# 960 unused matrix products of many shapes behind the needed ones, in a two-layer float32 trunk

## The chip, the core and the metric

The kernel runs on one core of one Trainium2 chip. Its engines are named as the profile names them: PE is TensorE (matmuls), PEld the loading of a matmul's stationary operand (its weights), DVE is VectorE, ACT ScalarE, POOL GpSimd, and SP issues DMAs. The metric is the device time of one execution in microseconds (us).

## The reference

Two post-LN residual layers on 272 tokens (16 learned meta tokens and 256 frames; the pad slots in front of them are masked and stay out of the kernel), with 2048 features. The first layer mixes by gated linear attention and stick-breaking attention, the second by a Mamba-2 scan. Cut to its frame:

```python
for layer in range(DEPTH):                      # DEPTH = 2
    if layer % 2 == 0:
        f = _even_mixer(h, valid, ...)          # h @ w_in, GLA and stick-breaking heads, gates, @ w_out
    else:
        f = _odd_mixer(h, valid, ...)           # h @ w_in, conv, chunked scan, gates, @ w_out
    ...                                         # h = layer norm of the residual sum
# the meta tokens are dropped: the output is (1, 256, 2048) float32
```

Nearly all arithmetic is in the four projections: 2048 features to some 10,000 columns and back in each layer, for 272 tokens.

## The kernel before

**Projections.** All weights are packed into units of 128 x 2048 numbers that are loaded one after the other (`raw`, three buffers), and each half of a unit is split into a high and a low part (`split_into`, L146 on ACT and L147 on DVE or POOL). Both parts have type float32r, in which PE takes a number with fewer bits. A float32 product is made of three float32r products: high by high, high by low, low by high. `three` (L164 to L166) issues them for the input projections and for layer 0's output projection, with 128 weight columns and 256 to 274 moving columns; `out1_half` (L422 to L424) issues them for layer 1's output projection with 512, and in the last two groups 256, moving columns. The activations lie in two row buffers, `xhi` and `xlo`, of 16 x 320 numbers per partition.

**Mixers.** Between the projections stand smaller products. Most of them have plain float32 operands, which PE takes apart by itself: such a matmul leaves two records in the trace and float32r one. Shapes are written as the profile writes them: `128*64 128x256` is 128 rows of contraction, 64 weight columns, and 256 moving columns.

**PSUM.** Eight banks of 512 float32 columns: four `pj` buffers for projections, two `po` buffers, and two fixed banks `z0`, `z1`.

**Order.** Mixers are generators that are pushed to a list and advanced one step (`tick`) between pieces of a projection. The framework then lists each engine's instructions by its own simulation, keeps dependences, and puts in the semaphore waits; a buffer that is taken again waits for the work on its former content.

**The end.** `tail` does the last four units of layer 1's output projection. For units 1 and 2 of them the split parts are put into `xhi` and `xlo`, whose content is no longer needed by then. Then it normalizes and stores the 256 tokens in two halves: `bn_stats` and the affine part on DVE, ACT and POOL, and DMAs to `out_h`.

At the start, before any data is there, ten products of constants are issued whose result is never read (L232).

Of the kernel before, what the change touches and what calls it, by code (L numbers as in the profile page):

```python
# [6 lines left out]
F32 = mybir.dt.float32  # L7
# [5 lines left out]
P = 128  # L13
# [54 lines left out]
NU = len(L0) + len(L1)  # L68
# [20 lines left out]
class _Body:  # L89
# [1014 lines left out]
    def tail(self):  # L1104

        nc, lp = self.nc, self.lp
        vec, pool = nc.vector, nc.gpsimd
        i0, g = NU - 4, NG - 1
        self.drain()
        self.load_unit(i0 + 2)  # L1110
        for n, dq in enumerate((1, 2)):
            for h in range(2):
                src = self.raw[i0 + dq][:, h * 1024 : (h + 1) * 1024]
                o = slice((2 * n + h) * 1024, (2 * n + h + 1) * 1024)
                hi, lo = [a.rearrange("p k t -> p (k t)")[:, o] for a in self.xrows]
                nc.scalar.activation(hi, src, AF.Copy)
                vec.tensor_tensor(lo, src, hi.bitcast(F32), op=ALU.subtract)
                self.parts[i0 + dq, h] = (hi, lo)
            if n == 0:
                self.load_unit(i0 + 3)  # L1120
        lg = self.hp.tile([P, D], F32, tag="hacc", name="lg")
        lb = lp.tile([P, D], F32, tag="M", name="lb")
        nc.sync.dma_start(lg, self.lnr_d[0].partition_broadcast(P))
        nc.sync.dma_start(lb, self.lnr_d[1].partition_broadcast(P))
        for h in range(2):
            self.split_half(i0 + 3, h)
        for t in range(2):
            st = lp.tile([P, 8, 6], F32, tag="fst", name=self.nm("fst"), bufs=2)
            acc = self.acc[:, t, :]
            for dq in range(4):  # L1130
                halves = (0, 1) if t == 1 and dq == 3 else (None,)
                for b in halves:
                    ps = self.pj()
                    for h in range(2):
                        self.out1_half(ps, g, t, *self.parts[i0 + dq, h], h, b)
                    self.out1_add(ps, g, t, dq, b)
                    with self.tc.high_priority():
                        for c in range(2) if b is None else (b,):
                            vec.bn_stats(st[:, 2 * dq + c, :], acc[:, dq * 512 + c * 256 : dq * 512 + (c + 1) * 256])
            mv = lp.tile([P, 2], F32, tag="fmv", name=self.nm("fmv"), bufs=2)  # L1140
            v, r, tm, mr = [lp.tile([P, 1], F32, tag=f"f{n}", name=self.nm("f"), bufs=2) for n in range(4)]
            with self.tc.high_priority():
                vec.bn_aggr(mv, st)
                vec.tensor_scalar(v, mv[:, 1:2], LN_EPS, None, op0=ALU.add)
                nc.scalar.activation(r, v, AF.Ln)
                nc.scalar.activation(r, r, AF.Exp, scale=-0.5)
                self.newton(r, v, tm)
                vec.scalar_tensor_tensor(mr, mv[:, 0:1], -1.0, r, op0=ALU.mult, op1=ALU.mult)
            cut = (0, 1024, 2048) if t == 0 else (0, 384, 1216, 2048)
            ch = [slice(a, b) for a, b in zip(cut, cut[1:])]  # L1150
            for cs in ch[1:]:
                vec.scalar_tensor_tensor(acc[:, cs], acc[:, cs], mv[:, 0:1], lg[:, cs], op0=ALU.subtract, op1=ALU.mult)
            a = acc[:, ch[0]]
            nc.scalar.activation(a, a, AF.Identity, bias=mr, scale=r)
            pool.tensor_tensor(a, a, lg[:, ch[0]], op=ALU.mult)
            pool.tensor_tensor(a, a, lb[:, ch[0]], op=ALU.add)
            for cs in ch[1:]:
                vec.scalar_tensor_tensor(acc[:, cs], acc[:, cs], r, lb[:, cs], op0=ALU.mult, op1=ALU.add)
                nc.sync.dma_start(self.out[t * P : (t + 1) * P, cs], acc[:, cs])
            nc.sync.dma_start(self.out[t * P : (t + 1) * P, ch[0]], a)  # L1160


def _pack(i):
# [53 lines left out]
```

## Time and profile before

| what | us |
|---|---|
| time, median of 2 runs | 1436.1 (1435.95 to 1436.24) |
| the profiled execution's own time | 1439.71 |
| its span, first to last instruction | 1437.6 |
| PE busy | 1418.9 (99%) |
| DVE busy | 984.4 (68%) |
| ACT busy | 761.5 (53%) |
| POOL busy | 350.1 (24%) |

The mean granted TensorE clock is 0.995 of full. In a row of the timeline the first number is the start in us from the span's start, the second the length in us; `x2` is two records in one row. A matmul's record is longer than its share of PE, since the next one starts before it ends: the distance from one start to the next is its cost in a dense sequence. In a row of the windows stand the stretch, its length, busy time and count of PE, PEld, DVE, ACT and POOL, then the granted TensorE clock, and the share and GB/s of DMA.

### The profile page before, as it was taken

Reading aid. Unit: us, or ns where it says so; the run is one execution under the profiler, and the core shown is the slowest. Engines: PE = TensorE matmul, PEld = TensorE weight load, DVE = VectorE, ACT = ScalarE, POOL = GpSimd, SP = SyncE. Lnnn points to the kernel's source line nnn. Section 1 sums busy time; section 2 is a strip of 40 time slices with the busy share of each in tenths; the row PEclk is TensorE's granted clock in tenths of the full one; section 3 lists DMA queues with packets and bytes.
Section 4 is the critical chain, followed back from the end, with each engine's and each line's share of the span. In section 5 each row is a group of like instructions: output and inputs, shape, how many; then the busy total and the mean of one; then the engine's idle time right before and its main releaser. Section 6 shows DMA issues by size and latency. Waiting matters only on the chain.

```text
span 1437.6 us, 26048 instructions
## 1 busy us (share of the span) xinstructions
PE 1418.9 (99%) x10780; PEld 1345.8 (94%) x10780; DVE 984.4 (68%) x1516; ACT 761.5 (53%) x1126; POOL 350.1 (24%) x297
## 2 busy tenths in 40 slices
PE   9999999999999999999999999999999999999996
PEld 7999999999999999999999999899898998989985
DVE  8647575575564465447799978577776767767677
ACT  5535454454345444445587666565555555555651
POOL 5010000100101110014401435333433433434333
PEclk9999999999999999999999999999999999999998
DMA  7544545445444445443446564554544556445551
GB/s 261 206 167 159 169 153 167 157 152 174 168 156 172 147 143 179 162 147 128 141 144 218 184 213 165 205 211 166 217 165 167 215 176 217 153 168 184 203 209 58
DMA packets 36566, 249.82 MB, mean 174 GB/s; under 512 B 4128, under 2 KB 4960, under 8 KB 7776
## 3 DMA queue, kind: packets, MB, share of 16 engines
q1 hardware_dynamic: 36304, 247.90, 49.4%
q8 instruction: 84, 1.38, 0.4%
q14 instruction: 34, 0.28, 0.1%
q10 hardware_dynamic: 144, 0.26, 0.1%
HBM read 245.94 MB, written 2.20 MB: 173 GB/s over the span
## 4 chain that ended last, share of the span: by engine, by line
PE 94%; DVE 3%; issue 1%; ACT 1%; POOL 1%; DMA 0%; POOLq 0%; SPq 0%; DVEq 0%
PE pj L164 24%; PE pj L166 24%; PE pj L165 24%; PE pj L422 4%; PE pj L423 4%; PE pj L424 4%; PE po L1070 1%; DVE wlo L147 1%; DVE xlo L737 1%; PE po L1072 1%; PE po L1023 1%; PE po L1074 0%; DMA raw<-in_wts 0%; ACT whi L146 0%; PE po L508 0%
## 5 line engine op out<-in xcount | busy, mean ns | idle before, releaser
L164 PE MATMUL pj<-xhi,whi 128*128 128x272 f32 (+4 forms) x2560 | 737.5, 288 | 3.9 <-DVE fix L815 2.5
L165 PE MATMUL pj<-xlo,whi 128*128 128x272 f32 (+4 forms) x2560 | 733.6, 287 | 0.0
L166 PE MATMUL pj<-xhi,wlo 128*128 128x272 f32 (+4 forms) x2560 | 733.1, 287 | 0.0
L147 DVE TENSOR_TENSOR wlo<-raw,whi 128x1024 fp32r<-128x1024 f32 (+1 forms) x402 | 511.3, 1275 | 289.2 <-ACT whi L146 288.1
L146 ACT ACTIVATE whi<-raw 128x1024 fp32r<-128x1024 f32 (+1 forms) x432 | 452.5, 1049 | 407.0 <-PE pj L165 344.1
L164 PEld LDWEIGHTS pj<-xhi,whi 128*128 128x128 f32 x2560 | 483.5, 189 | 8.4 <-DVE fix L815 2.9
L165 PEld LDWEIGHTS pj<-xlo,whi 128*128 128x128 f32 x2560 | 482.6, 189 | 2.1 <-DVE xlo L293 0.7
L166 PEld LDWEIGHTS pj<-xhi,wlo 128*128 128x128 f32 x2560 | 482.3, 188 | 2.2 <-DVE xlo L293 1.3
L164 PE MATMUL pj<-mixh,whi 128*128 128x272 f32 x384 | 111.6, 292 | 0.0
L165 PE MATMUL pj<-mixl,whi 128*128 128x272 f32 x384 | 110.5, 288 | 0.0
L166 PE MATMUL pj<-mixh,wlo 128*128 128x272 f32 x384 | 110.2, 287 | 0.0
L147 POOL TENSOR_TENSOR wlo<-raw,whi 128x1024 fp32r<-128x1024 f32 x30 | 75.2, 2508 | 136.0 <-ACT whi L146 136.0
L422 PE MATMUL pj<-whi,yh 128*128 128x512 f32 (+1 forms) x244 | 97.3, 399 | 0.0
L423 PE MATMUL pj<-wlo,yh 128*128 128x512 f32 (+1 forms) x244 | 94.9, 389 | 0.0
L424 PE MATMUL pj<-whi,yl 128*128 128x512 f32 (+1 forms) x244 | 94.3, 386 | 0.0
L253 POOL TENSOR_TENSOR gr<-gr,gsc 128x1088 f32<-128x1088 f32 x6 | 15.5, 2578 | 290.4 <-ACT gsc L252 290.4
L165 PEld LDWEIGHTS pj<-mixl,whi 128*128 128x128 f32 x384 | 72.3, 188 | 0.3
L164 PEld LDWEIGHTS pj<-mixh,whi 128*128 128x128 f32 x384 | 72.1, 188 | 0.5
L166 PEld LDWEIGHTS pj<-mixh,wlo 128*128 128x128 f32 x384 | 72.3, 188 | 0.1
L431 DVE SCALAR_TENSOR_TENSOR acc<-pj,rr,acc 128x512 f32<-128x512 f32 (+1 forms) x65 | 47.4, 737 | 28.4 <-PE pj L424 28.2
L1078 POOL TENSOR_TENSOR yu<-yu,gz 128x256 f32<-128x256 f32 x32 | 44.0, 1382 | 84.6 <-DVE yu L1077 77.5
L424 PEld LDWEIGHTS pj<-whi,yl 128*128 128x128 f32 x244 | 45.9, 188 | 9.8
(305 smaller groups left out, 1519.1 us busy)
## 6 DMA issues: line engine op xcount, KB each, us to landing
raw<-in_wts SPq DMA_DIRECT2D x214, 1024.0 KB, 4.8
ebc<-edr SPq DMA_DIRECT2D x8, 1664.0 KB, 6.9
hacc<-in_xT SPq DMA_DIRECT2D x8, 272.0 KB, 6.3
raw<-in_wts SPq DMA_DIRECT2D x8, 256.0 KB, 5.3
lg<-in_lnr SPq DMA_DIRECT2D x1, 1024.0 KB, 4.4
lb<-in_lnr SPq DMA_DIRECT2D x1, 1024.0 KB, 5.9
out_h<-acc SPq DMA_DIRECT2D x2, 512.0 KB, 2.6
out_h<-acc SPq DMA_DIRECT2D x2, 416.0 KB, 2.5
```

Of the source, the lines that this page charges most:

```text
L146: self.nc.scalar.activation(hi, src, AF.Copy)
L147: eng.tensor_tensor(lo, src, hi.bitcast(F32), op=ALU.subtract)
L164: mm(ps, whi, xhi, start=first, stop=False)
L165: mm(ps, whi, xlo, start=False, stop=False)
L166: mm(ps, wlo, xhi, start=False, stop=last)
L253: mul(c, c, e, op=ALU.mult)
L422: mm(ps, yh[:, kk, tt], hi[:, k, :], start=kk == 0, stop=False)
L423: mm(ps, yh[:, kk, tt], lo[:, k, :], start=False, stop=False)
L424: mm(ps, yl[:, kk, tt], hi[:, k, :], start=False, stop=kk == 3)
L431: self.nc.vector.scalar_tensor_tensor(a, ps, r[:, t : t + 1], a, op0=ALU.mult, op1=ALU.add)
L737: vec.scalar_tensor_tensor(self.xlo[:, d, :T], x, g, self.xhi[:, d, :T].bitcast(F32), op0=ALU.mult, op1=ALU.subtract)
L1078: nc.gpsimd.tensor_tensor(u, u, z[:, j, :], op=ALU.mult)
```

## The change

`tail` calls a new method, `rest`, as its last step. It issues 960 matmuls in 53 groups ("patterns"). A group takes one `po` buffer (or two) and makes `rep` = 6 times three products (the last group 8 times three), each with operands that lie in SBUF already: weights are slices of the last unit's high and low part (`wh`, `wl`), moving operands slices of the row buffers (`xh`, `xl`). Nothing reads the results. `n` is the number of moving columns, `kk` of rows (contraction), `m` of weight columns; `po` is the first PSUM column, `xo` the place of the moving operand in its row; `blk` takes the moving operand in two pieces, `two` writes the result in two pieces; `f32` takes the operands as plain float32; `alt` puts the results into the lower and the upper 64 PSUM partitions in turn.

```diff
             nc.sync.dma_start(self.out[t * P : (t + 1) * P, ch[0]], a)
+        self.rest()
+
+    def rest(self):
+
+        mm = self.nc.tensor.matmul
+        xh, xl = [a.rearrange("p k t -> p (k t)") for a in self.xrows]
+        wh, wl = self.parts[NU - 1, 0]
+
+        def pattern(n, xo=48, kk=P, m=P, po=0, banks=1, alt=False, two=0, f32=False, rep=6, blk=None, xp=320, mp=0):
+            pss = [self.po() for _ in range(banks)]
+            for k in range(rep):
+                hi, lo = [t[:kk, k * P : k * P + m] for t in (wh, wl)]
+                p, q = [t[:kk, xo + k * xp : xo + k * xp + n] for t in (xh, xl)]
+                if blk:
+                    p, q = [
+                        t[:kk, xo + k * xp : xo + k * xp + blk[1] * 2].rearrange("p (a b) -> p a b", a=2)[:, :, : blk[0]]
+                        for t in (xh, xl)
+                    ]
+                for i, (s, v) in enumerate([(hi, p), (hi, q), (lo, p)]):
+                    if f32:
+                        s, v = s.bitcast(F32), v.bitcast(F32)
+                    c = 3 * k + i
+                    r = slice(64 * (c % 2), 64 * (c % 2) + m) if alt else slice(mp, mp + m)
+                    o = pss[c % banks][r, po : po + n]
+                    if two:
+                        o = pss[0][r, po : po + 2 * two].rearrange("p (a b) -> p a b", a=2)[:, :, : n // 2]
+                    elif blk:
+                        o = o.rearrange("p (a b) -> p a b", a=2)
+                    mm(o, s, v, start=c < 2, stop=c >= 3 * rep - 2, skip_group_check=True)
+
+        for n in (16, 32, 64, 128, 144, 160, 192, 208, 224, 240, 248, 254):
+            pattern(n)
+        for xo in (0, 16, 32):
+            pattern(144, xo=xo)
+        for n, kk in ((144, 16), (144, 48), (144, 80), (272, 16), (272, 80), (16, 16), (16, 80)):
+            pattern(n, kk=kk)
+        for n, m in ((16, 16), (144, 16), (272, 16), (144, 64), (256, 64)):
+            pattern(n, m=m)
+        for po in (16, 64, 112, 128, 176, 240):
+            pattern(272, po=po)
+        pattern(272, banks=2)
+        pattern(256, banks=2)
+        pattern(512, xo=0, xp=512, banks=2)
+        pattern(272, blk=(136, 144))
+        pattern(272, blk=(136, 160), xp=384)
+        pattern(272, two=144)
+        pattern(272, two=160)
+        for n in (16, 64, 128, 144, 256, 272):
+            pattern(n, f32=True)
+        for n, m in ((144, 64), (256, 64)):
+            pattern(n, m=m, f32=True, alt=True)
+        for n, kk in ((16, 16), (16, 64), (144, 16), (144, 64)):
+            pattern(n, kk=kk, f32=True)
+        pattern(272, rep=8)
```

On DVE, ACT, POOL and SP the instructions are the same as before. PE's queue ended, before, with the last products of the output projection (`pj`, the numbers are buffers) and a branch.

```order
L424 MATMUL pj_15657<-whi_15500,yl_15128 128x256
L422 MATMUL pj_15657<-whi_15504,yh_15127 128x256
L423 MATMUL pj_15657<-wlo_15505,yh_15127 128x256
L424 MATMUL pj_15657<-whi_15504,yl_15128 128x256
L1212 UNCONDITIONAL_BRANCH
```

In the changed kernel the same products are followed by `rest`; the waits of an instruction stand in brackets, and PE_49 is PE's own semaphore.

```order
L422 MATMUL pj_15657<-whi_15504,yh_15127 128x256
L423 MATMUL pj_15657<-wlo_15505,yh_15127 128x256
L424 MATMUL pj_15657<-whi_15504,yl_15128 128x256
L1189 MATMUL po_15695<-xhi,whi_15500 128x16 [waits PE_49]
L1189 MATMUL po_15695<-xlo,whi_15500 128x16
L1189 MATMUL po_15695<-xhi,wlo_15501 128x16
```

All 960 stand behind the last needed product, and only the first product into a buffer has a wait. Of the groups with two buffers, the queue of the changed kernel has this at the change from the first buffer to the second.

```order
L1189 MATMUL po_16322<-xhi,whi_15500 128x272
L1189 MATMUL po_16322<-xhi,wlo_15501 128x272
L1189 MATMUL po_16322<-xlo,whi_15500 128x272
L1189 MATMUL po_16323<-xlo,whi_15500 128x272
L1189 MATMUL po_16323<-xhi,whi_15500 128x272
L1189 MATMUL po_16323<-xhi,wlo_15501 128x272
```

The code takes the two buffers in turn; the queue has nine products into the first and then nine into the second.

## The prediction

> **What bounds the kernel now.** The page comes first, for what the span is made of.
>
> ```profile
> span 1437.6 us, 26048 instructions
> PE 1418.9 (99%) x10780; PEld 1345.8 (94%) x10780; DVE 984.4 (68%) x1516; ACT 761.5 (53%) x1126; POOL 350.1 (24%) x297
> PE 94%; DVE 3%; issue 1%; ACT 1%; POOL 1%; DMA 0%; POOLq 0%; SPq 0%; DVEq 0%
> ```
>
> PE is busy for 99% of the span and 94% of the chain that ended last is PE. Whatever stands on PE's queue is paid in full, unless it falls where PE would be idle. The timeline of the last 12 us shows the one large stretch of that kind.
>
> ```profile
> 1426.15 0.28 PE L424 MATMUL pj<-whi,yl 128*128 128x256 f32 x1
> ...
> 1426.39 0.28 PE L423 MATMUL pj<-wlo,yh 128*128 128x256 f32 x1
> ...
> 1426.51 0.28 PE L424 MATMUL pj<-whi,yl 128*128 128x256 f32 x1
> 1426.83 0.48 DVE L431 SCALAR_TENSOR_TENSOR acc<-pj,rr,acc 128x256 f32<-128x256 f32 x1 [0.48 <-PE pj L424]
> ...
> 1434.62 0.33 SPq L1160 DMA_DIRECT2D out_h<-acc  x1
> ```
>
> PE's last matmul starts at 1426.51 and ends at 1426.8; the other engines then normalize and store until 1437.6. That is 10.8 us without PE work. The run behind this profile took 1439.71 us, 2.1 more than its span and 3.6 more than the median of 1436.1.
>
> **The change part by part.** Nothing is removed or moved. 960 matmuls stand behind the last one on PE, and no instruction is added on another engine. Their operands (xhi, xlo, and the last unit's whi and wlo) are complete when PE's own last products have read them. The only new waits are PE's on itself: the first product into a PSUM buffer waits for the group that used that buffer before, at least nine products earlier, so the awaited one has ended by the time its turn comes; I cost them at nothing (a wait that did bite would cost one drain, about the 0.28 us of a record, for 56 of them 16 us at most). So the added work starts at 1426.63, a step of 0.12 after the last one, and the tail's 10.8 us run beside it.
>
> A record's length is no cost here, because matmuls overlap; I use the step from one start to the next, from the timeline of one stretch of layer 0 and one of layer 1. A float32 product leaves two records (x2), a float32r product one.
>
> ```profile
> 449.64 0.62 PE L675 MATMUL z<-sq,sk 128*128 128x272 f32 x2
> 450.10 0.41 PE L676 MATMUL z<-sq,sk 128*128 128x144 f32 x2
> ```
>
> ```profile
> 456.95 0.29 PE L694 MATMUL z<-s0h,nL_r 128*128 128x272 f32 x1
> 457.07 0.29 PE L164 MATMUL pj<-xhi,whi 128*128 128x272 f32 x1
> ...
> 458.19 0.41 PE L696 MATMUL z<-ppad,nones 128*128 128x144 f32 x2
> 458.44 0.41 PE L697 MATMUL z<-ppad,nL 128*128 128x144 f32 x2
> 458.78 0.39 PE L698 MATMUL z<-ppad,nones 16*128 16x16 f32 x2
> 459.02 0.37 PE L699 MATMUL z<-ppad,nones 16*128 16x16 f32 x2
> 459.32 0.21 PE L700 MATMUL z<-ppad,nL 16*16 16x16 f32 x2
> 459.46 0.40 PE L166 MATMUL pj<-xhi,wlo 128*128 128x272 f32 x1
> ```
>
> ```profile
> 780.09 0.28 PE L165 MATMUL pj<-xlo,whi 128*128 128x256 f32 x1
> 780.20 0.28 PE L166 MATMUL pj<-xhi,wlo 128*128 128x256 f32 x1
> ...
> 780.57 0.59 PE L976 MATMUL z<-bc 128*128 128x256 f32 x2
> 781.00 0.41 PE L977 MATMUL z<-bc 128*128 128x144 f32 x2
> ```
>
> ```profile
> 856.38 0.65 PE L1070 MATMUL po<-M,xd 128*64 128x256 f32 x4
> 856.86 0.41 PE L1072 MATMUL po<-M,xd 128*64 128x144 f32 x4
> 857.21 0.29 PE L1074 MATMUL po<-mt,xd 16*64 16x16 f32 x4
> ```
>
> ```profile
> 1404.72 0.39 PE L422 MATMUL pj<-whi,yh 128*128 128x512 f32 x1
> 1404.95 0.39 PE L423 MATMUL pj<-wlo,yh 128*128 128x512 f32 x1
> ```
>
> Steps: float32r with 272 columns 0.124 us (nine products from 457.07 to 458.19, and 0.12 for L694 at PSUM column 16), 256 columns 0.11 to 0.12, 512 columns 0.23. Float32: 272 columns 0.46, 256 columns 0.43, 144 columns 0.25. The page has no float32r product below 256 columns, so the largest group has to be bounded.
>
> - Float32r, 128 weight columns, 16 to 254 columns, any rows: 20 groups of 18, 360 products. Streaming alone would fall with the columns: 0.46 ns a column from the 272-column step. But L698 and L699 stream 16 columns and take 0.24 for two records, 0.12 each, as much as a 256-column step, while L700 with the same 16 columns and 16 weight columns takes 0.14 for two with a change of form in it. What differs is the weights: loading 128 weight columns takes about 0.11 to 0.12, and it limits every product whose streaming is shorter. Lower end: weights for nothing, N x 0.46 ns. Upper end: the price of a float32 product of the same width. I take 0.115, between L699's 0.12 and the 0.11 of 780.09 to 780.20, since all of these load 128 weight columns: 41.4 us.
> - Float32r, 256 columns and more, all weight columns: 258 products with 272 columns x 0.124, 18 with 256 x 0.12, 18 with 512 x 0.225: 38.2 us. In them are PSUM places, split operands and two banks, which I cost at nothing: L694 writes at column 16 for the usual 0.12. The order issues a two-bank group as nine products into one buffer and then nine into the other, so it is no alternation.
> - Float32r with 16 or 64 weight columns: 16 columns 0.07 (L700), 144 columns 0.075, the rest as above: 8.3 us.
> - Float32, 128 rows: 16, 64 and 128 columns at two weight loads of 0.12, 144 at 0.25, 256 at 0.43, 272 at 0.46, 18 each: 33.4 us.
> - Float32 with 64 weight columns, halves in turn: L1070 does two in 0.48, L1072 two in 0.35; 9 pairs each: 7.5 us.
> - Float32 with 16 and 64 rows: 36 with 16 columns x 0.24, 36 with 144 x 0.25: 17.6 us. If small row groups can't load weights beside a running product, each 144-column or 272-column one is dearer by a load: some 13 us over all groups with few rows; I take none of it.
>
> Sum 146.4, with some changes of form (L697 to L698 is 0.34 where a pair of records is 0.25) 147 us. PE then ends at 1426.6 + 147 = 1573.6, plus 0.8 for the drain and the program's end: span 1574.4, profiled 1576.5, median 3.6 less, **1573**.
>
> On PSUM the Trainium skill (PSUM — Partial Sum Buffer, Specifications (TRN2)) says that any non-contiguous pattern slows matmuls significantly. By it the two groups that write two halves of 136 columns would cost more; at twice the step that is an estimate of 4.5 us on top. No row here writes such a pattern.
>
> One term is missing. The sum assumes the full clock, and the windows around the change of layers show when it isn't granted.
>
> ```profile
> 702.30:705.70 3.40, 3.40 (x29) 3.40 (x28) 3.40 (x4) 1.25 (x2) 1.80 (x2) 1.00 0.31 51
> 705.70:709.10 3.40, 1.89 (x10) 1.06 (x9) 2.39 (x6) 2.52 (x5) 0.00 (x0) 1.00 0.61 258
> 709.10:712.50 3.40, 3.40 (x14) 2.73 (x13) 1.65 (x3) 2.18 (x4) 0.00 (x0) 0.50 0.70 178
> 712.50:716.00 3.50, 3.50 (x26) 3.38 (x26) 0.07 (x2) 1.06 (x2) 0.00 (x0) 1.00 0.32 131
> ```
>
> ```profile
> 706.67 0.34 PE L164 MATMUL po<-xhi,whi 128*64 128x274 f32 x1 [0.64 <-ACT xhi L736]
> 707.20 0.34 PE L165 MATMUL po<-xlo,whi 128*64 128x274 f32 x1 [0.19 <-DVE xlo L737]
> 707.38 0.29 PE L166 MATMUL po<-xhi,wlo 128*64 128x274 f32 x1
> 708.35 0.34 PE L164 MATMUL po<-xhi,whi 128*64 128x274 f32 x1 [0.68 <-ACT xhi L736]
> 708.52 0.62 PE L769 MATMUL po<-ssum,ones 128*128 128x272 f32 x2
> ```
>
> Between 705.7 and 709.1 ten records (at 0.12 to 0.23 of streaming each, some 1.2 to 1.6 us of 3.4) fell into a window, with no idle longer than 0.68; the next window had half the clock, and after a full one it came back. At a floor of 0.115 a 16-column product streams 0.007 us, 6%; 32 columns 13%, 64 columns 26%. Weight loads keep PE's row full, but if the gate counts streaming, those groups halve the clock. They are: 16, 32 and 64 columns at the start (6 us), 16 columns with 16 and 80 rows and with 16 weight columns (5 us), float32 16 columns (4 us), and 16 columns with few rows (9 us): 24 us that double, less about 3.4 us at each of four entries, since the clock falls a window late, plus 1.7 us at each exit, where busy work runs a window at half: 24 - 14 + 7 = 17 us. I take it: 1573 + 17 = **1590**.
>
> **The rivals.**
> - The clock stays full. For it: weight loads fill PE in those groups, whereas 705.70 to 709.10 had only 1.06 us of them. Time 1573. The Trainium skill (TensorE: Matmul & The Clock Gate, HAM oscillation — how this bites in real kernels) gives the rule as no idle gaps of PE above about 3.4 us; by that rule nothing here would drop the clock, though the window above lost it with gaps of 0.68.
> - Narrow float32r is no single pass. No row excludes it that below 256 columns a product costs what float32 does. Then the twelve widths rise by 42 us (16 to 128 columns to 0.23, 144 to 0.25, above that 1.68 ns a column, which is L675's 0.46 over 272), the other groups below 256 by 25: 67 us, time 1640, with the clock up to 1655. Against it: only that widths from 256 to 274 cost one pass.
> - Weights load for nothing and narrow products cost their streaming (at least 0.04): 23 us less, time 1550. L698 and L699 speak against it.
> - The other side: not slower. The results are never read, and a program could lose them; or they could fit beside the tail. To stay within 2% (28.7 us) with 10.8 us of cover, a product may cost (28.7 + 10.8) / 960 = 0.041 us; it decides above that, and only 16 weight columns come near. Against dropping: the ten products at the start are never read either, and all run:
>
> ```profile
> 1.06 4.64 PE L232 MATMUL po<-ones 128*128 128x128 f32 x20 [1.06 <-POOL ones L218]
> ```
>
> Time if dropped 1436.
>
> **How the numbers follow.** Forecast 0.33, full clock 0.30, four-pass price 0.28, free weights 0.05, not slower 0.03; 0.01 is left for something dearer. The time is the likeliest's, 1590. The range 1560 to 1655 takes in the first three with the 13 us for few rows; left out are free weights, not slower and the top of the four-pass case. A change is told from none at about 2%, 28.7 us: slower 0.97, same 0.02, faster 0.01.
>
> **What would show it.** In the profile after, PE goes on from 1426.6 without gaps while the tail ends near 1437 as before, and the chain's end is PE. Under my account float32r rows from 16 to 240 columns step by one same 0.11 to 0.12, one record each, and the granted clock falls to 0.5 within 7 us of 1426. Steps that grow with the columns, to 0.4 at 254, or two records for a product, are the four-pass price; a clock of 1.0 throughout is the first rival. Steps under 0.1 at 16 columns would break the weight floor, and gaps at every 18th product would show the waits.

## The result and the profile after

The changed kernel takes 1613.59 us (1613.01 to 1614.16), against 1436.1 before: 1.1224 times the time before, 95% interval 1.1200 to 1.1249, 177.5 us more. The forecast was 1590 with a range of 1560 to 1655. The page of the changed kernel:

```profile
span 1612.1 us, 28400 instructions
PE 1604.0 (100%) x11956; PEld 1523.7 (95%) x11956; DVE 985.5 (61%) x1516; ACT 761.3 (47%) x1126; POOL 347.2 (22%) x297
PEclk9999999999999999999999999999999999977985
PE pj L164 22%; PE pj L166 21%; PE pj L165 21%; PE po L1189 12%; PE pj L422 4%; PE pj L423 4%; PE pj L424 4%; PE po L1070 1%; DVE wlo L147 1%; DVE xlo L737 1%; PE po L1072 0%; PE po L1023 0%; PE po L1074 0%; ACT whi L146 0%; DMA raw<-in_wts 0%
```

DVE, ACT and POOL did what they did before. PE has 1176 records more: 960 products, of which the 216 float32 ones leave two records each and the 744 float32r ones, narrow or not, leave one. The last five slices of the granted clock are at 7, 7, 9, 8 and 5 tenths; all earlier ones are at nine tenths or more. The timeline where the added work begins, the tail's last store, and the last product:

```profile
1422.98 0.28 PE L424 MATMUL pj<-whi,yl 128*128 128x256 f32 x1
1423.10 0.17 PE L1189 MATMUL po<-xhi,whi 128*128 128x16 f32 x1
...
1423.24 0.26 PE L1189 MATMUL po<-xhi,wlo 128*128 128x16 f32 x1
1423.35 0.26 PE L1189 MATMUL po<-xhi,whi 128*128 128x16 f32 x1
...
1431.11 0.33 SPq L1160 DMA_DIRECT2D out_h<-acc  x1
...
1610.92 0.28 PE L1189 MATMUL po<-xhi,wlo 128*128 128x272 f32 x1
```

A product of 16 columns steps by 0.11 us. The added work runs from 1423.1 to 1611.2, 188.1 us in which PE is never idle, while the tail's last store is issued at 1431.1. Next come windows of the changed kernel, L1189 alone (stretch, length, busy time and records of PE and PEld, granted clock, DMA share and GB/s): the whole of the added work, and then stretches that each lie within one group.

```profile
1423.10:1611.20 188.10, 188.10 (x1176) 180.14 (x1176) 0.75 0.02 9
1423.10:1425.00 1.90, 1.90 (x18) 1.90 (x19) 1.00 0.00 0
1427.80:1431.60 3.80, 3.80 (x20) 3.80 (x20) 0.50 0.42 172
1435.50:1439.30 3.80, 3.80 (x19) 3.80 (x19) 0.50 0.00 0
1446.90:1448.90 2.00, 2.00 (x20) 2.00 (x20) 1.00 0.00 0
1457.30:1463.20 5.90, 5.90 (x55) 5.90 (x53) 1.00 0.01 3
1472.00:1476.30 4.30, 4.30 (x18) 4.05 (x18) 0.50 0.00 0
1476.40:1480.60 4.20, 4.20 (x18) 4.03 (x18) 0.50 0.00 0
1520.00:1529.00 9.00, 9.00 (x75) 9.00 (x73) 1.00 0.00 0
1597.30:1605.80 8.50, 8.50 (x36) 8.25 (x35) 0.50 0.01 2
```

Over all, the clock is 0.75. In the groups, in order: 16 columns at full clock; 64 columns and 144 columns at half clock, 0.213 a product; 208 columns at full clock, 0.112; 144 columns again, now at full clock and 0.111; 272 columns with 16 and then with 80 rows at half clock, 0.227; the operands and results in two pieces, 0.125; float32 144 columns with 64 rows at half clock. Two things are not in the prediction: 144 columns run at either clock, and 272 columns with few rows, which stream without a pause, stay at half.

### The profile page after: what moved, and what is told of

Its sections match the earlier page's. It is cut to its first block, busy times and chain, and to the rows that moved or that the text cites. A ratio compares the mean times of both kernels' runs of the same rounds, so it can differ in the third digit from the quotient of the medians.

```text
span 1612.1 us, 28400 instructions
## 1 busy us (share of the span) xinstructions
PE 1604.0 (100%) x11956; PEld 1523.7 (95%) x11956; DVE 985.5 (61%) x1516; ACT 761.3 (47%) x1126; POOL 347.2 (22%) x297
## 4 chain that ended last, share of the span: by engine, by line
PE 95%; DVE 2%; issue 1%; ACT 1%; POOL 0%; DMA 0%; SPq 0%; DVEq 0%; POOLq 0%
PE pj L164 22%; PE pj L166 21%; PE pj L165 21%; PE po L1189 12%; PE pj L422 4%; PE pj L423 4%; PE pj L424 4%; PE po L1070 1%; DVE wlo L147 1%; DVE xlo L737 1%; PE po L1072 0%; PE po L1023 0%; PE po L1074 0%; ACT whi L146 0%; DMA raw<-in_wts 0%
## 5 line engine op out<-in xcount | busy, mean ns | idle before, releaser
L1189 PE MATMUL po<-xhi,whi 128*128 128x272 f32 (+27 forms) x392 | 118.0, 338 | 0.0
L1189 PE MATMUL po<-xhi,wlo 128*128 128x272 f32 (+27 forms) x392 | 116.8, 334 | 0.0
L1189 PE MATMUL po<-xlo,whi 128*128 128x272 f32 (+27 forms) x392 | 116.6, 334 | 0.0
L1189 PEld LDWEIGHTS po<-xhi,whi 128*128 128x128 f32 (+6 forms) x392 | 84.6, 229 | 4.0 <-issue 1.8
L1189 PEld LDWEIGHTS po<-xhi,wlo 128*128 128x128 f32 (+6 forms) x392 | 85.3, 230 | 1.9
L1189 PEld LDWEIGHTS po<-xlo,whi 128*128 128x128 f32 (+6 forms) x392 | 85.0, 230 | 1.9
```

What stands on the lines that cost most here:

```text
L1189: mm(o, s, v, start=c < 2, stop=c >= 3 * rep - 2, skip_group_check=True)
```

## The experiments

The theory on record is that a gate counts streaming in 3.4 us windows and halves the clock after a window of too little. Its rivals are a price of the forms themselves, and for the few-row groups a late return of the clock. In all experiments but the last `rest` is edited and the needed work in front of it stays as it is, so the output doesn't depend on them.

**The same products in another order.** In blocks of nine (three times the three products of a step of `rep`), those that stream little and wide ones take turns, whichever brings the share of streaming back to its mean. In the code `weight` is an estimate of a product's streaming time, weighed with its rows, and of the time that it takes, and `share` is the first over the second. Every product starts its own sum, and one buffer serves where a group had two.

```diff
             for k in range(rep):
+                todo.append((k, n, xo, kk, m, po, alt, two, f32, blk, xp, mp))
...
+        todo.sort(key=lambda t: (share(t), t[3]))
...
+        while todo:
+            low = done >= 0
+            for _ in range(min(3, len(todo))):
+                t = todo.pop(0 if low else -1)
+                issue([self.po()], *t)
+                done += weight(t)[0] - total * weight(t)[1]
```

> The same 960 products in another order: three by three, those that stream little (few columns, few rows) in turn with wide ones, so that every 3.4 us window holds about the same share of streaming, some 60%; only PSUM buffers and start flags differ. Theory 1, the clock gate counts streaming and halves the clock after a window of too little: the granted clock stays at 1.0 to the end, the added work falls from 188 us to about 140 to 155 (changes of form cost some), the run takes 1565 to 1585 us. Theory 2, the narrow and few-row forms are dear by themselves whatever stands around them: about 1613 us as with the groups in a row, or more for the changes of form.

It took 1578.94 us (1576.30 to 1582.19), 1.0981 times before (1.0959 to 1.1003), some 35 us less than with the groups in a row. The window over the whole of the added work (here and below busy time of PE alone, unless said):

```profile
1423.20:1573.20 150.00, 150.00 (x1177) 0.99 0.03 11
```

The same 960 products take 150 us at a clock of 0.99 where they took 188 at 0.75. At full clock that is 150 x 0.99 = 148 us against 188.1 x 0.75 = 141. Much of the 7 us between stands at changes of form, of which the mixed order has many more (a product of 272 columns behind one with 16 rows steps by 0.233 where 0.124 is usual). So the clock made the difference, and the narrow and few-row forms have no price of their own beyond the floor of 0.112. Two executions at a mean clock of 0.999 took 1576.3 and two at 0.995 and 0.996 took 1582, so even this order lost some windows; in the profile it is one, at 1450.3.

**All rows.** One line more in `pattern`, so that every group has 128 rows.

```diff
+            kk = P
             pss = [self.po() for _ in range(banks)]
```

> The changed kernel with all 128 rows in every group; columns, weight columns and order stay. Theory 1, the gate weighs streaming with the rows in use: the groups of 144 and 272 columns with 16 to 80 rows no longer keep the clock down, the stretches at half clock from 1467 to 1494 and after 1576 shrink to what the 16-column groups cause, and the run takes 1588 to 1603 us. Theory 2, rows don't count, and the clock comes back late after a drop for another reason: 1612 to 1615 us.

1593.44 us (1588.43 to 1594.56), 1.1072 times before (1.1049 to 1.1096): 20 us less than the changed kernel, by giving the array more to do.

```profile
1424.10:1590.20 166.10, 166.10 (x1178) 0.85 0.03 10
```

166.1 x 0.85 is again 141 us. So at full clock rows hardly alter the price of these products; they alter what the gate sees, and the rival falls.

**Rows, from full clock.** In place of the 960 products, as in all runs below but the last: stretches of 96 products of 272 columns, each after 120 with all rows.

```diff
+        for kk in (16, 32, 48, 64, 80, 96, 112, 120):
+            pattern(272, rep=40)
+            pattern(272, kk=kk, rep=32)
```

> In place of the 960 products: 96 float32r products of 272 columns with 16, 32, 48, 64, 80, 96, 112 and 120 rows, each stretch after 120 with all rows. Streaming time is the same in all. Theory 1, rows count: the clock falls to 0.5 within two windows for 16, 32 and 48 rows (13 to 38% of the array's rows), and stays at 1.0 for 80 rows and more (63%); 64 rows is open. Theory 2, streaming time alone counts: 1.0 throughout, and a step of 0.124 us everywhere.

16, 32 and 48 rows halved the clock, 64 to 120 kept it. The windows within 48, 64 and 80 rows:

```profile
1513.90:1528.70 14.80, 14.80 (x66) 0.50 0.00 1
1546.50:1558.20 11.70, 11.70 (x96) 1.00 0.00 0
1573.40:1585.00 11.60, 11.60 (x96) 1.00 0.01 1
```

**Columns, from full clock.** The same with all rows and 32 to 144 columns.

```diff
+        for n in (32, 64, 80, 96, 104, 112, 120, 128, 144):
+            pattern(272, rep=40)
+            pattern(n, rep=32)
```

> In place of the 960 products: 96 float32r products with all rows and 32, 64, 80, 96, 104, 112, 120, 128 and 144 columns, each stretch after 120 of 272 columns. The step is 0.112 us at full clock in all, so the share of streaming is 12, 24, 30, 36, 39, 42, 45, 48 and 54%. Theory: the clock falls to 0.5 for 32 and 64 columns, stays at 1.0 for 144, and changes over at one width between 80 and 128. If weight loading counted too, it would stay at 1.0 for all.

32 to 96 columns halved it, 104 and more kept it; the windows within 96 and 104 columns, with all engines (PEld's is the second):

```profile
1539.50:1552.40 12.90, 12.90 (x63) 12.90 (x62) 0.00 (x0) 0.00 (x0) 0.00 (x0) 0.50 0.00 0
1569.30:1579.80 10.50, 10.50 (x97) 10.50 (x95) 0.00 (x0) 0.00 (x0) 0.00 (x0) 1.00 0.01 2
```

Weight loading fills PEld in both, so it isn't what the gate counts. At 0.1116 a product, 30.6 fit into a window of 3.41 us (the clock's changes lie at multiples of that in every trace): 96 columns are 2940 streamed columns in a window, 104 are 3180. For 48 rows it is 27.5 products x 272 x 48 / 128 = 2800. At half clock 192 columns, the width that brought the clock back in the changed kernel, are 16 x 192 = 3072. That made one number likely, some 3000 columns in a window at either clock, and the next runs test it.

**Back from half clock, by columns.** 72 products of 16 columns to halve the clock, then 96 of one width.

```diff
+        for n in (144, 160, 168, 176, 184, 192, 208):
+            pattern(272, rep=40)
+            pattern(16, rep=24)
+            pattern(n, rep=32)
```

> In place of the 960 products: for each of 144, 160, 168, 176, 184, 192 and 208 columns 120 products of 272 columns, then 72 of 16 columns, which halve the clock, then 96 of that width. One threshold in streamed columns per 3.4 us window, some 3000 to 3070 as the widths 96 and 104 and the recovery after 192 columns put it: at half clock a product of up to 256 columns takes 0.213 us, 16 in a window, so 144 to 184 columns (2304 to 2944) stay at half to their end, 208 (3328) comes back after one window, 192 (3072) is at the edge. Rival, the share of streaming in the window must exceed the same 36 to 39% at either clock: all seven come back within two windows.

144 to 184 columns stayed at half for their whole 20.5 us; 192 came back after the first window that was all theirs, and so did 208. Windows within 184 columns, and within 192 before and after the return:

```profile
1646.00:1664.20 18.20, 18.20 (x87) 0.50 0.00 1
1695.20:1698.50 3.30, 3.30 (x18) 0.50 0.03 5
1698.60:1705.90 7.30, 7.30 (x68) 1.00 0.00 0
```

144 columns keep a full clock (the run before) and can't get it back: at half clock the same products stream half as many columns in a window, 2304.

**Back from half clock, by rows.**

```diff
+        for kk in (80, 88, 96, 104, 112, 128):
+            pattern(272, rep=40)
+            pattern(16, rep=24)
+            pattern(272, kk=kk, rep=24)
```

> As the runs on columns, but from the low side and with rows: after 72 products of 16 columns have halved the clock, 72 products of 272 columns with 80, 88, 96, 104, 112 and 128 rows. At half clock some 4096 columns stream in a window; weighed with rows of 128 that is 2560, 2816, 3072, 3328, 3584 and 4096. One threshold near 3000 to 3070: 80 and 88 rows stay at half, 104 and more come back after one window, 96 is at the edge. If rows counted in row groups of 32 or 64, 80 and 88 would behave as 96 or as 128.

80 and 88 rows stayed at half, 96 and more came back. Windows within 88 rows, and within 96 after the return:

```profile
1495.60:1511.60 16.00, 16.00 (x72) 0.50 0.00 1
1546.00:1551.60 5.60, 5.60 (x48) 1.00 0.01 3
```

88 and 96 rows differ, so rows count one by one and not in groups of 32 or 64.

**Columns and rows and passes together.**

```diff
+        for n, kk, f32 in ((192, 64, False), (208, 64, False), (256, 48, False), (48, P, True), (56, P, True), (144, 80, False), (144, 96, False)):
+            pattern(272, rep=40)
+            pattern(n, kk=kk, f32=f32, rep=16 if f32 else 32)
```

> From full clock, combinations: float32r 192 and 208 columns with 64 rows, 256 with 48 rows, 144 with 80 and with 96 rows, and float32 with 48 and 56 columns and all rows. If the gate counts columns x passes x rows / 128 in a window of 3.4 us with a threshold near 3000: 192 x 64 (2940), 256 x 48 (2780), 144 x 80 (2750) and float32 48 (4 x 48 in 0.224: 2925) drop to half; 208 x 64 (3180), 144 x 96 (3300) and float32 56 (3410) keep 1.0. If rows and columns had thresholds of their own (50% of rows, 104 columns), 192 x 64, 144 x 80 and both float32 groups would keep 1.0 and only 256 x 48 would drop.

A float32 product is counted as four passes: in the changed kernel each of its two records with 256 columns steps by 0.216 us, near the 0.227 of a float32r product with 512 columns, where 256 columns of float32r step by 0.118. All seven went as the product of columns, passes and rows says. Windows within them, in the order of the code:

```profile
1444.80:1456.40 11.60, 11.60 (x56) 0.50 0.00 0
1474.20:1484.70 10.50, 10.50 (x96) 1.00 0.01 2
1506.20:1515.00 8.80, 8.80 (x43) 0.50 0.01 2
1536.90:1548.70 11.80, 11.80 (x57) 0.50 0.00 0
1566.10:1576.60 10.50, 10.50 (x97) 1.00 0.01 2
1594.90:1608.80 13.90, 13.90 (x67) 0.50 0.00 1
1625.60:1636.10 10.50, 10.50 (x97) 1.00 0.00 0
```

**Weights.**

```diff
+        for m in (16, 32, 48, 64, 96, 128):
+            pattern(272, rep=40)
+            pattern(16, m=m, rep=6)
+        for m in (16, 64):
+            pattern(272, rep=40)
+            pattern(272, m=m, rep=32)
+        for m in (16, 32, 64, 128):
+            pattern(272, rep=40)
+            pattern(16, m=m, f32=True, rep=6)
```

> In place of the 960 products, each after 120 products of 272 columns: 18 float32r products of 16 columns with 16, 32, 48, 64, 96 and 128 weight columns, 96 of 272 columns with 16 and with 64 weight columns, 18 float32 products of 16 columns with 16, 32, 64 and 128 weight columns. Theory, loading the weights sets the floor: steps at full clock of about 0.027, 0.03, 0.042, 0.056, 0.083 and 0.112 us, two such for a float32 product; the 272-column stretches keep the clock at 1.0, since weight columns don't count for the gate. Rival, a floor of its own for few moving columns: 0.11 for all from 32 weight columns up; and if the gate counted cells in use, 16 weight columns would halve the clock.

Timeline of PE, the first product of a group of 18 and the first after it, for 16, 64 and 128 weight columns:

```profile
1439.72 0.17 PE L1178 MATMUL po<-xhi,whi 128*16 128x16 f32 x1
...
1440.20 0.37 PE L1178 MATMUL po<-xhi,whi 128*128 128x272 f32 x1
...
1486.22 0.17 PE L1178 MATMUL po<-xhi,whi 128*64 128x16 f32 x1
...
1487.24 0.37 PE L1178 MATMUL po<-xhi,whi 128*128 128x272 f32 x1
...
1518.49 0.17 PE L1178 MATMUL po<-xhi,whi 128*128 128x16 f32 x1
...
1520.41 0.37 PE L1178 MATMUL po<-xhi,whi 128*128 128x272 f32 x1
```

18 products take 0.48, 1.02 and 1.92 us; the steps inside the groups are 0.027, 0.032, 0.045, 0.058, 0.085 and 0.112 from 16 to 128 weight columns, about 0.83 ns for each further weight column from 32 up, and a float32 product has two such records. The floor is the weights' loading. 272 columns with 16 or 64 weight columns kept a clock of 1.0, so weight columns don't count for the gate. The one window at half clock in the added work, 1643.0 to 1646.4, follows the 3.9 us of float32 products with 16 columns and 128 weight columns, enough to fill most of a window.

**Filling a wait of the kernel before.** The one practical use at hand: the profile of before loses a window at the change of layers. Ten unused products go where PE waits there.

```diff
+            if k >= KT - 2:
+                spare = self.pj()
+                for n in range(5):
+                    mm(spare[:, :T], self.parts[len(L0), 0][0][:, :P], self.xrows[0][:, n, 32 : 32 + T], start=True, stop=True)
             self.in_kt(self.ps_dt[:64, :TG], hi[:, k, :], lo[:, k, :], k, 0, TG)
```

> The kernel before, not the changed one, with two times five unused products of 272 columns put where PE waits at the change of layers (in norm0, ahead of the last two steps of dt's projection). In the profile of before the window from 705.7 to 709.1 streamed some 2760 columns there, under the threshold of about 3000, and the next window ran at half clock, which costs up to 1.7 us. With 2720 columns more the window stays above it wherever it falls: the granted clock is 1.0 over the change of layers, and the run is 0 to 1.7 us faster than before, less what the ten products (1.24 us) delay where the wait is shorter than they are. If the drop there has another cause, the window of half clock stays in some executions and the time is equal or up to 1.2 us longer.

1440.03 us, 1.0015 times before (1.0006 to 1.0024): slower by 0.15%. PE in its timeline there:

```profile
705.90 0.80 PE L770 MATMUL pj<-xhi,whi 128*128 128x272 f32 x5
706.74 0.34 PE L164 MATMUL po<-xhi,whi 128*64 128x274 f32 x1
708.00 0.34 PE L165 MATMUL po<-xlo,whi 128*64 128x274 f32 x1 [0.92 <-DVE xlo L737]
```

In the profiled execution the clock stays full over the change of layers, but a wait of 0.92 us for DVE remains behind the filling, and another window, from 831.6, ran at half. PE stands still ahead of it:

```profile
831.27 0.85 PE L1027 MATMUL po<-ident,xt 128*128 128x128 f32 x4 [2.24 <-POOL xt L929]
```

The profile of before has no such wait; from 765 to 900 us its longest on PE is 0.35. So in this execution the window that was won at the change of layers is lost again at 831.6, and the wait comes on top. Why POOL is late there isn't shown; the added products also change the order of what follows on PE. The median is 2.4 us longer, where the expected gain was at most 1.7.

## Why the prediction was right, and where it was off

- **Nothing hides the work, and it starts behind the last product.** Right: 1423.1 is 0.12 after the last needed product, and the tail ran beside it. The start was put at 1426.63 and came 3.5 us earlier: the profiled execution of before had two windows at half clock, at 9.4 and at 709.1, worth up to 1.7 us each, and the one of the changed kernel had none before 1426. Set side by side, product by product, the two traces are 0.6 us apart ahead of 9.4 (a first wait for ACT of 1.36 against 0.77), 1.6 ahead of 709.1 and 3.0 behind that window; the last 0.5 comes between 836 and 847 at full clock, and its cause isn't shown. That also fits the 3.6 us by which that execution was over the median.
- **The waits cost nothing.** Right: the seven groups of 272 columns from 1498.2 to 1513.8, six at other PSUM columns and one in two buffers, step by 0.12 to 0.13 throughout, at their starts too.
- **The weight floor.** Right, and the largest term: 0.112 where 0.115 was taken, one record a product, up to 240 columns. The four-pass rival is out, as is that of free weights.
- **The sum at full clock.** 147 forecast, 141 measured (188.1 x 0.75, and 166.1 x 0.85). The excess of 6 is spread: each group's time multiplied by its clock comes out about 1.2 us lower in narrow float32r, 1.6 with few weight columns (0.07 taken for 16 columns, 0.027 measured), 1.1 in float32 with all rows (0.24 taken for 16 columns, 0.223 measured), 1.2 in the halves in turn and 0.8 in float32 with few rows. The 13 us held back for few rows were not needed: float32 with 144 columns and few rows steps by 0.240 a record at half clock, twice the 0.122 of all rows at full, so no load is added there.
- **Two pieces in PSUM.** The Trainium skill (PSUM — Partial Sum Buffer, Specifications (TRN2)) says that non-contiguous patterns slow matmuls significantly. Here results in two runs of 136 columns step by 0.123 (1524.5 to 1529), as in one piece, so nothing was added; shorter runs were not tried. A moving operand in two pieces steps by 0.126 (1520 to 1524.5).
- **The clock.** The mechanism, streaming counted in windows, was right but incomplete, and the term was mis-sized: 17 us forecast, 188.1 - 141 = 47 measured. The step that failed is the list of groups "that double", which took only those that stream little by columns, and the exit, which was given one window. Rows count as columns do, so 144 columns with 16 and 48 rows halved the clock at 1467.2, and 272 columns with 16 and 80 rows and float32 144 columns with few rows stayed at half; and coming back takes the same number of columns out of half as many, so 64 to 160 columns stayed there after the 16-column group had brought them to it. The rival of the full clock is out, and with it the rule of the Trainium skill (TensorE: Matmul & The Clock Gate, HAM oscillation — how this bites in real kernels) as a sufficient one: here PE had no gap at all, and ran half of the added time at half clock.

The two errors, start and sum, took 3.5 and 6 us off the forecast where the clock added 30, and the median lies 1.5 over the profiled span where 1.5 under it was taken; the range held the time because it was drawn for a rival, not for this.

## What to carry to other kernels

Narrow products in a row cost their weight load, 0.112 us for 128 weight columns whatever the columns up to 240, and 0.213 once they have halved the clock; few rows halve it as few columns do. Mix them with wide ones instead of putting them in blocks: the same products gained 35 us of 177 by order alone. A wide product directly behind a narrow block isn't enough if it has few rows or, with float32r and 128 weight columns, under 192 columns; it takes a full window of dense work to get the clock back.

## What the runs showed of the hardware

One number describes all drops and returns in the runs built for it: moving columns x passes x rows / 128, summed over a window of 3.41 us. At 2940 and 2944 the next window was at half clock, at 3072 and 3180 at full, and this holds from either clock (of products of 272 columns some 7480 columns fit into a window at full clock and 4095 at half). Weight columns and weight loading don't count. The number also fits where nothing was built for it: of some 5150 windows after 13 us in the eleven profiles, with PE's records counted in this way, a float32 one as two passes, 188 are followed by half clock, none of them with over 2980, and no other has under 3020; so the threshold lies between these. That holds for the needed work too, idle time included. The window from 705.7 in the profile of before has some 2790 and lost the clock; at the same change of layers, in the run on rows from half clock, the windows fall 0.4 us later, the one from 706.1 has some 3120, and the clock stayed. With 128 weight columns and all rows, a float32r stream of 104 to 184 columns should therefore keep the clock that it finds: 104 to 144 columns were seen to hold a full clock, 144 to 184 not to regain it, and 144 both.
